# 24 feature weight units split by transfers: the high part cast by one transfer, the low part as minus the high part with the weights added by a second

## The chip, the core and the metric

The kernel runs on one core of a Trainium2 chip. A core has a matrix engine (PE), a vector engine (DVE), a scalar engine (ACT), a general engine (POOL) and an engine that mostly issues transfers (SP). Each of them works through its own list of instructions in order, and waits at an instruction until the semaphores that it names have come. Transfers run beside them on 16 DMA engines, and are issued here from SP's queue and from POOL's.

The metric is the device time of one execution in microseconds (us). Three timed runs of the kernel before took 497.48, 497.65 and 499.13 us; the median is 497.65 us.

## The reference, cut to what matters

Two layers, each a normalisation, one wide projection of 512 tokens, four mixing groups that work on slices of that projection, and one output projection, which is added to the stream. All of it is float32.

```python
def hybrid_layer(x, positions, norm_g, w_in, ...):
    h = rmsnorm(x, norm_g)
    p = h @ w_in
    (cq, ckv, kr, g_a, c_h, c_b, c_c, g_b, sg_u, sg_v, g_c, mq, mk, mv, g_d) = jnp.split(p, offs, axis=-1)
    ...
    o_b = c_b * short_conv(c_c * c_h, conv_w)
    o_c = spatial_gate(sg_u, sg_v, sg_ln_g, sg_ln_b, sg_w, sg_b)
    ...
    y = jnp.concatenate([o_a * jax.nn.silu(g_a), o_b * jax.nn.silu(g_b),
                         o_c * jax.nn.silu(g_c), o_d * jax.nn.silu(g_d)], axis=-1)
    return y @ w_out
```

`w_in` is 1024 x 3488 in each layer. The change concerns the columns of `c_h`, `c_c`, `c_b`, `g_b` and `g_d` (both halves of 128 columns of each) and the second halves of `sg_u` and `g_c`: twelve blocks of 1024 x 128 weights in a layer, 24 in all.

## The kernel before, in words

**Products in two parts.** PE works in a shortened float32 format (fp32r). To keep the precision, each operand is held as a high part (the value rounded to fp32r) and a low part (the value minus its high part), and `mm3` (L254) makes each product of three matrix multiplications: high by high, high by low, low by high.

**Weight units.** The weights come in units (class `Unit`, L271) of up to 128 partitions x 1024 float32, 512 KB. Their order is fixed in `order`: in a layer c0 to c3, uq, ukv, then the list `SEQ` (L338): sq (four units), ga0, ga1, kv (four units), su0, gc0, ch0, cc0, gd0, gd1, cb0, gb0, ch1, cc1, cb1, gb1, su1, gc1; then the units of the output projection (`ZPROD`, L43). A feature unit such as ch0 serves 24 matrix multiplications of 128 x 512, one accumulation over eight slices of 128 rows.

**Loading and splitting.** Two generators go through `order`. `load_units` (L360) takes a raw buffer (there are two, `NRAW`; a few units borrow a buffer of another pool) and issues the load from SP (L265). `split_units` (L378) waits for the load, takes one of six pairs of buffers `whi`, `wlo` (`wS`, L246, `NW`), and for each half of 512 columns makes the high part (a copy on ACT, or on DVE when DVE is well ahead) and the low part (a subtraction on DVE), then gives the raw buffer back. As long as a unit isn't wanted soon (`unit`, L401, marks the next four), a half is only put in where ACT and DVE have nothing planned. A pair of buffers comes free when PE has made its last product with it (`done_unit`, L1338). During the four passes of the kv units (one for each block of 128 tokens) those four units hold four of the six pairs; PE gives them back in the last pass.

**The order of the work.** The program is written by a planner that runs while the kernel is built (class `Order`, L67, class `Chain`, L151). Each piece of work is a generator; the planner keeps a clock of planned time for ACT ("A"), DVE ("V"), POOL ("G") and the DMA engines ("D"), and PE's planned time is `now`. An instruction is put on its engine's list when its inputs are planned to be there (at most 300 ns ahead, `SLACK`), and the planned prices are those in the methods of `Chain`: for instance a transfer issued from SP takes its bytes divided by 360 bytes per ns on the DMA clock, and 2000 ns more until it has landed (L262). At run time the lists are fixed, and an engine whose next instruction isn't ready waits, with all that stands behind it.

**What else stands on the lists near the change.** POOL computes reciprocal roots (`pow_rstd`, L587) and the rotary steps (`rope`, L635) of the token groups, zeroes halves of key tiles (L1204), and issues the transfers of `t_sums` (L318). `t_sums` makes sums of quadrants of the output weights in DRAM in four steps in each layer: a copy issued from SP (L324), then an accumulating transfer issued from POOL (L330). It is spawned at a planned 36 us in the first layer, and after the sq units in the second. The attention heads of the two attention groups (`heads`, L1108) run among the feature units: a product on PE, a maximum on DVE, an exponential on ACT, transposes on PE, a split on ACT and DVE, a product on PE.

Of the kernel before, what the change touches and what calls it, by code (L numbers as in the profile page):

```python
# [11 lines left out]
F32 = mybir.dt.float32  # L12
F32R = mybir.dt.float32r
I32 = mybir.dt.int32
AF = mybir.ActivationFunctionType
ALU = mybir.AluOpType
AX = mybir.AxisListType

P = 128
S = 512  # L20
NT = S // P
D = 1024
# [19 lines left out]
K0, K1, KK = (2, 3, 0, 1), (4, 5, 6, 7), (0, 2, 3, 1)  # L42
ZPROD = ("b11", "t3", "b21", "t4", "t2", "t1", "b22")  # L43
TS0 = 36000.0
TAIL = ((0, 256), (256, 512))

C_CQ, C_KV, C_GA, C_CH, C_CB, C_CC, C_GB = 0, 256, 416, 672, 928, 1184, 1440
# [153 lines left out]
def hybrid_trunk(ctx: ExitStack, tc: tile.TileContext, x, positions, norm_g, w_c, w_f, w_t, w_o, mla_q_norm_g,  # L201
                 mla_w_uq, mla_kv_norm_g, mla_w_ukv, mla_q_g, mla_k_nope_g, mla_k_rope_g, conv_w,
                 sg_ln_g, sg_ln_b, sg_w, sg_b, moba_q_g, moba_k_g, out):
    nc = tc.nc
    V, A, G, PE = nc.vector, nc.scalar, nc.gpsimd, nc.tensor
# [16 lines left out]
    o = Order()  # L222
# [39 lines left out]
    def dma(ch, nbytes, dst, src):  # L262

        o.clk["D"] = max(o.clk["D"], ch.t) + nbytes / 360.0
        nc.sync.dma_start(dst, src)  # L265
        ch.t = o.clk["D"] + 2000.0
# [4 lines left out]
    class Unit:  # L271
        def __init__(self, src, a, b, name):
            self.src, self.a, self.b, self.name = src, a, b, name
            self.loaded, self.ready, self.wanted = Event(), Event(), False
            self.slots = eS if name[:-2] in EARLY else wS

        def view(self):
            n = self.a * self.b
            return (self.hi[:, :n].rearrange("p (a b) -> p a b", a=self.a),
                    self.lo[:, :n].rearrange("p (a b) -> p a b", a=self.a))  # L280
# [15 lines left out]
    def add_unit(*a):  # L296
        u = Unit(*a)
        units[u.name] = u
        u.idx = len(order)
        order.append(u)  # L300
# [8 lines left out]
    tsum_ev = {(l, n, j): Event() for l, n in tsum for j in range(2)}  # L309
# [8 lines left out]
    def t_sums(l):  # L318

        for steps in ((("t1", "b11", "b12"), ("t3", "b12", "b22")), (("t2", "t1", "b22"),), (("t4", "t2", "b21"),)):  # L320
            for n, a, _ in steps:
                for j in range(2):
                    o.clk["D"] = max(o.clk["D"], o.now) + 1500.0
                    nc.sync.dma_start(z_src(l, n, j), z_src(l, a, j))  # L324
                    yield o.now + 4000.0
            yield o.now + 4000.0
            for n, _, b in steps:
                for j in range(2):
                    o.clk["G"] = max(o.clk["G"], o.now) + 1000.0
                    nc.gpsimd.dma_start(z_src(l, n, j), quad(l, b, j), accum_op=ALU.add, max_dma_last_dim=1024)  # L330
                    o.set(tsum_ev[l, n, j], o.now + 10000.0)
                    yield o.now + 4000.0
            yield o.now + 8000.0
# [6 lines left out]
    for l in range(DEPTH):  # L340
# [15 lines left out]
        for half in range(2):  # L356
            for kq in WORDER:
                add_unit(w_o[l, half, kq], 2, 512, f"wo{half}{kq}_{l}")

    def load_units():  # L360
        for u in order:
            ch = Chain(o)
            u.raw_slots = rawS
            if u.name in ("c2_0", "c3_0") or u.name[:-3] in ZPROD and u.name[-3] == "1":
                u.raw_slots = tkS
                u.raw = (yield from tkS.get(ch, f"raw_{u.name}", 96)).rearrange("p a b c -> p (a b c)")
            else:
                u.raw = yield from rawS.get(ch, u.name)
            key = (int(u.name[-1]), u.name[:-3], ord(u.name[-3]) - 48)
            if key in tsum_ev:  # L370
                yield from ch.wait(tsum_ev[key])
            dma(ch, P * u.a * u.b * 4, u.raw[:, :u.a * u.b], u.src)
            o.set(u.loaded, ch.t)
            for e in LOAD_HOOKS.pop(u.name, ()):
                e()
            yield o.now

    def split_units():  # L378
        for u in order:
            ch = Chain(o)  # L380
            yield from ch.wait(u.loaded)
            u.hi, u.lo = yield from u.slots.get(ch, u.name)
            n = u.a * u.b
            for i in range(2):
                while ch.t > o.now + SLACK:
                    yield ch.t - SLACK
                while not u.wanted and max(o.clk["A"], o.clk["V"]) > o.now + WSLACK:
                    yield o.now + 100.0
                sl = slice(i * n // 2, (i + 1) * n // 2)
                c2 = Chain(o, max(o.now, ch.t))  # L390
                hi, lo, raw = u.hi[:, sl], u.lo[:, sl], u.raw[:, sl]
                if o.clk["V"] + 600.0 < o.clk["A"]:
                    yield from c2.dve_fast(V.tensor_copy, hi, raw)
                else:
                    yield from c2.act(A.activation, hi, raw, AF.Copy)
                yield from c2.dve(V.tensor_tensor, lo, raw, hi.bitcast(F32), op=ALU.subtract)
            ch.t = c2.t
            u.raw_slots.put(ch)
            o.set(u.ready, ch.t)
# [890 lines left out]
    def z_out(L, n, i, a, t0, ev, put, c0=0, c1=512):  # L1290

        ch = Chain(o, t0)
        for t, half, op, done in {"t3": ((2 + i, 1, ALU.subtract, False),), "b21": ((i, 0, ALU.add, True),),
                                  "t4": ((2 + i, 0, ALU.add, False),), "t2": ((2 + i, 0, ALU.subtract, True),),
                                  "t1": ((2 + i, 1, ALU.add, True),), "u": ((i, 1, ALU.add, False),),
                                  "b22": ((i, 1, ALU.add, True),)}[n]:
            yield from ch.wait(L.xr[t])
            xx = L.x[t][:, half * 512 + c0:half * 512 + c1]
            k = dict(in0=xx, in1=a[:, c0:c1]) if op == ALU.subtract else dict(in0=a[:, c0:c1], in1=xx)
            yield from ch.dve(V.tensor_tensor, out=xx, op=op, **k)  # L1300
            if done and (c0, c1) != (0, 512):
                nc.sync.dma_start(out[0, t * P:(t + 1) * P, half * 512 + c0:half * 512 + c1], xx)
            elif done:
                if n == "t2":
                    yield from ch.wait(L.s4[i])
                if n in ("t1", "t2") and L.l < DEPTH - 1:
                    junk_ = yield from trS.get(ch, f"jk{t}{half}")
                else:
                    junk_ = a
                yield from row_done(L, t, half, ch.t, junk_)  # L1310
                if n in ("t1", "t2") and L.l < DEPTH - 1:
                    trS.put(ch)
        o.set(ev, ch.t)
        if n == "t4":
            o.set(L.s4[i], ch.t)
        if put:
            put(ch)


    def main():  # L1320
# [21 lines left out]
        def seven(L):  # L1342
# [37 lines left out]
            for n in ZPROD:  # L1380
                for i in range(2):
# [7 lines left out]
                    if (l, n, i) == (DEPTH - 1, "b22", 1):  # L1389
                        ev2 = Event()  # L1390
                        yield from z_out(L, "u", i, a, m.t, ev2, sS.put)
                        for c0, c1 in TAIL:
                            a = yield from accS.get(m, f"ot{c0}_{l}")
# [18 lines left out]
        for L in layers:  # L1412
# [49 lines left out]
            for half in range(0 if L.seven else 2):  # L1462
                us = {}

                def part(t, a, i0, i1, c0=0, c1=512):
                    for i in range(i0, i1):
                        k = YORDER[i]
                        yield from m.wait(L.y[k])
                        if k // 2 not in us:
                            us[k // 2] = yield from unit(m, f"wo{half}{k // 2}_{l}")  # L1470
                        wh, wlo = us[k // 2]
                        yh, yl = y_tiles(L, k)
                        yield from mm3(m, c1 - c0, a[:, c0:c1], yh[:, t * P:(t + 1) * P], yl[:, t * P:(t + 1) * P],
                                       wh[:, k % 2, c0:c1], wlo[:, k % 2, c0:c1], i == 0, i == KT - 1)
                        if t == NT - 1 and c1 == 512 and all(x // 2 != k // 2 for x in YORDER[i + 1:]):
                            done_unit(f"wo{half}{k // 2}_{l}")
                        yield o.now

                acc = {}
                for group, cut in (((0, 1, 2), YCUT), ((3,), 0)) if half == 0 else (((t,), 0) for t in range(NT)):  # L1480
                    for i0, i1 in ((0, cut), (cut, KT)):
                        for t in group:
# [4 lines left out]
                            if (l, half, t) == (DEPTH - 1, 1, NT - 1):  # L1487
                                for c0, c1 in TAIL:
                                    yield from part(t, acc[t], i0, i1, c0, c1)
# [18 lines left out]
    def start():  # L1508
# [27 lines left out]
        LOAD_HOOKS["ukv_0"] = (lambda: load_params(L0),)  # L1536
        L0.par_t = 17500.0
        o.spawn(load_units(), None, 4)
        o.spawn(split_units(), None, 5)
        o.spawn(rope_tables(), ROPET, 6)  # L1540
        o.spawn(main(), None, 10)
# [22 lines left out]
    if 0 in SEVEN:  # L1564
        o.spawn(t_sums(0), TS0, 4)
    o.spawn(start())
# [51 lines left out]
```

## Time and profile before

| what | value |
|---|---|
| timed runs | 497.48, 497.65, 499.13 us, median 497.65 us |
| the profiled execution's own time | 499.12 us |
| its span, from the first to the last instruction | 497.4 us |
| granted clock of PE over it, as a share of the full one | 1.0 |
| hardware queue, issued from SP | 73.10 MB |
| software queue, issued from POOL | 8.39 MB |

The profiled execution's own time is 1.7 us above its span, and 1.5 us above the median of the timed runs.

How to read the lines of the profile that follow. L188 is line 188 of the kernel; since the planner's helpers record nearly all instructions, most of ACT, DVE and POOL stands at L162 and nearly all of PE at L188, and groups are told apart by their tiles ("wlo_cc<-raw_cc,whi_cc" writes a low part from a raw buffer and its high part). Engines: PE (its weight loads are PEld), DVE, ACT, POOL, SP; a "q" behind an engine's name is its queue of issues. Busy PE is the union of modelled matrix multiplications, which overlap, so it can hide short gaps. "Idle before" is the time that the engine stood before instructions of a group, with what ended most of it.

### The profile page before, as it was taken

How to read it: one execution, taken by the hardware profiler on the slowest of the kernel's cores; microseconds unless marked ns; L12 is line 12 of the kernel's file. 1: busy time of each engine (PE TensorE's matmuls, PEld its weight loads, DVE VectorE, ACT ScalarE, POOL GpSimd, SP SyncE). 2: the span in 40 equal slices, each digit the busy share in tenths (PEclk: the TensorE clock that was granted, in tenths of full speed). 3: DMA queues.
4: the chain of work that ended last, by engine and by line, in shares of the span. 5: the costliest groups of instructions: out<-in, count | busy, mean ns of one | idle time of the engine just before them, and what ended most of it. 6: DMA issues, size and time to landing. Idle time of an engine off the chain costs nothing.

```text
span 497.4 us, 7832 instructions
## 1 busy us (share of the span) xinstructions
PE 486.4 (98%) x2448; PEld 412.5 (83%) x2448; DVE 386.0 (78%) x1008; ACT 317.0 (64%) x933; POOL 156.2 (31%) x328
## 2 busy tenths in 40 slices
PE   6899999999999999999999999999999999999997
PEld 4798878788888888888889988888888888888886
DVE  4877884777988788669898698677969788765992
ACT  5688753576777775446657896567758587524640
POOL 6867883656110000000031388463351000000000
PEclk9999999999999999999999999999999999999999
DMA  8545559444575235786474232664548528565642
GB/s 273 150 141 199 196 117 203 171 86 88 192 145 188 71 98 175 210 299 219 157 256 157 86 106 108 211 149 97 118 122 245 142 102 215 174 249 188 227 171 92
DMA packets 35339, 81.98 MB, mean 165 GB/s; under 512 B 7137, under 2 KB 16609, under 8 KB 35042
## 3 DMA queue, kind: packets, MB, share of 16 engines
q1 hardware_dynamic: 26818, 73.10, 42.7%
q0 software_dynamic: 8480, 8.39, 11.5%
q8 instruction: 19, 0.31, 0.3%
q14 instruction: 22, 0.18, 0.1%
HBM read 73.61 MB, written 24.64 MB: 198 GB/s over the span
## 4 chain that ended last, share of the span: by engine, by line
PE 87%; POOL 4%; ACT 3%; DMA 3%; DVE 2%; issue 1%; POOLq 0%; DVEq 0%
PE kv L188 7%; PE cq L188 6%; PE oy L188 6%; PE sq L188 5%; PE cb L188 4%; PE gd L188 4%; PE ch L188 4%; PE cc L188 4%; PE su L188 4%; PE gc L188 4%; PE gb L188 4%; PE ox L188 4%; PE oz L188 4%; PE sa L188 3%; PE ga L188 2%; PE od L188 2%
## 5 line engine op out<-in xcount | busy, mean ns | idle before, releaser
L162 ACT ACTIVATE pd<-pd,mnd 128x256 f32<-128x256 f32 (+3 forms) x50 | 26.9, 547 | 2.8 <-DVE mnd L162 2.3
L330 POOL DMA_DIRECT2D t<-in_w_o_dram x16 | 17.9, 1121 | 33.1 <-DMA t<-t 22.6
L162 ACT ACTIVATE pha<-pTa 128x512 fp32r<-128x512 f32 (+3 forms) x32 | 13.9, 436 | 20.0 <-PE pTa L188 19.8
L188 PE MATMUL kv<-whi_kv,hTh 128*128 128x512 f32 x64 | 26.1, 408 | 0.0
L188 PE MATMUL kv<-whi_kv,hTl 128*128 128x512 f32 x64 | 25.1, 392 | 0.0
L188 PE MATMUL kv<-wlo_kv,hTh 128*128 128x512 f32 x64 | 25.0, 391 | 0.0
L188 PE MATMUL cq<-whi_c,hTh 128*128 128x416 f32 x64 | 24.0, 376 | 0.0
L162 ACT ACTIVATE phd<-pTd 128x512 fp32r<-128x512 f32 (+3 forms) x32 | 13.8, 434 | 14.9 <-PE pTd L188 14.7
L162 ACT ACTIVATE pa<-pa,mna 128x256 f32<-128x256 f32 (+3 forms) x40 | 21.4, 542 | 2.5 <-DVE mna L162 2.4
L188 PE MATMUL cq<-whi_c,hTl 128*128 128x416 f32 x64 | 22.6, 353 | 0.0
L188 PE MATMUL cq<-wlo_c,hTh 128*128 128x416 f32 x64 | 22.5, 351 | 0.0
L162 DVE TENSOR_TENSOR wlo_t<-raw_t,whi_t 128x512 fp32r<-128x512 f32 x32 | 21.1, 691 | 0.0
L162 ACT ACTIVATE whi_t<-raw_t 128x512 fp32r<-128x512 f32 x32 | 18.2, 618 | 4.1 <-DMA raw_t<-t 4.1
L162 POOL TENSOR_SCALAR xss<-xss 128x1 f32<-128x1 f32 x8 | 3.8, 476 | 52.3 <-ACT jk L162 45.1
L162 DVE TENSOR_TENSOR pla<-pTa,pha 128x512 fp32r<-128x512 f32 (+3 forms) x32 | 15.2, 484 | 5.5 <-ACT pha L162 5.5
L188 PE MATMUL sq<-yTh,hTh 128*128 128x512 f32 x48 | 18.9, 393 | 0.0
L188 PE MATMUL sq<-yTh,hTl 128*128 128x512 f32 x48 | 18.7, 390 | 0.0
L162 DVE TENSOR_TENSOR pld<-pTd,phd 128x512 fp32r<-128x512 f32 (+3 forms) x32 | 15.2, 484 | 4.5 <-ACT phd L162 4.4
L188 PE MATMUL sq<-yTl,hTh 128*128 128x512 f32 x48 | 18.7, 390 | 0.0
L162 DVE CUSTOM_DVE_ANT_0 pa<-sa,maskb 128x512 f32<-128x512 f32 (+3 forms) x32 | 14.8, 484 | 5.0 <-PE pTa L188 4.2
L162 DVE TENSOR_TENSOR wlo_b<-raw_b,whi_b 128x512 fp32r<-128x512 f32 x24 | 16.0, 688 | 0.7 <-ACT whi_b L162 0.7
L162 DVE CUSTOM_DVE_ANT_0 pd<-sd,maskb 128x256 f32<-128x256 f32 (+3 forms) x32 | 15.0, 483 | 2.0 <-PE pTd L188 1.9
(377 smaller groups left out, 1853.0 us busy)
## 6 DMA issues: line engine op xcount, KB each, us to landing
t<-in_w_o_dram POOLq DMA_DIRECT2D x16, 512.0 KB, 6.2
raw_t<-t SPq DMA_DIRECT2D x16, 512.0 KB, 4.0
raw_b<-in_w_o_dram SPq DMA_DIRECT2D x12, 512.0 KB, 4.2
raw_sq<-in_w_t_dram SPq DMA_DIRECT2D x8, 512.0 KB, 3.5
t<-in_w_o_dram SPq DMA_DIRECT2D x8, 512.0 KB, 4.4
raw_kv<-in_w_t_dram SPq DMA_DIRECT2D x8, 512.0 KB, 3.6
t<-t SPq DMA_DIRECT2D x8, 512.0 KB, 4.8
ys<-ysc SPq DMA_DIRECT2D x14, 256.0 KB, 5.2
```

Of the source, the lines that this page charges most:

```text
L162: f(*a, **k)
L188: f(*a, **k)
L330: nc.gpsimd.dma_start(z_src(l, n, j), quad(l, b, j), accum_op=ALU.add, max_dma_last_dim=1024)
```

## The change

Units whose name is in a new list `BY_DMA` (twelve names, so 24 units in the two layers) are no longer loaded into a raw buffer from SP, and no longer split by copies and subtractions. `load_units` skips them. `split_units` takes the pair of buffers for such a unit in its turn, as before, and starts a generator `unit_by_dma` for it. That issues, from POOL, a transfer of the weights from DRAM straight into `hi`, casting float32 to fp32r on the way; when it is planned to have landed, one ACT instruction writes minus `hi` into `lo` (128 x 1024, where before there were halves); then POOL issues a second transfer of the same weights, which is added onto `lo`. The planner's prices for these are in `pool_dma`: 1000 ns on POOL's clock for an issue, the bytes divided by 360 bytes per ns on the DMA clock (twice the bytes for the accumulating one), and 2500 ns until it has landed. The wait for `t_sums` in `load_units` moves to a helper, `sum_done`, unchanged in what it does; the units in `BY_DMA` never have such a wait.

```diff
+BY_DMA = ("ch0", "cc0", "gd0", "gd1", "cb0", "gb0", "ch1", "cc1", "cb1", "gb1", "su1", "gc1")
...
             self.slots = eS if name[:-2] in EARLY else wS
+            self.by_dma = name[:-2] in BY_DMA
...
+    def sum_done(ch, u):
+        key = (int(u.name[-1]), u.name[:-3], ord(u.name[-3]) - 48)
+        if key in tsum_ev:
+            yield from ch.wait(tsum_ev[key])
+
+    def pool_dma(ch, nbytes, *a, **k):
+
+        yield from ch._emit("G", 1000.0, nc.gpsimd.dma_start, a, k)
+        o.clk["D"] = max(o.clk["D"], ch.t) + nbytes / 360.0
+        ch.t = o.clk["D"] + 2500.0
+
+    def unit_by_dma(u, ch):
+
+        n = u.a * u.b
+        hi, lo = u.hi[:, :n], u.lo[:, :n]
+        yield from sum_done(ch, u)
+        yield from pool_dma(ch, P * n * 4, hi, u.src)
+        yield from ch.act(A.activation, lo, hi.bitcast(F32), AF.Copy, scale=-1.0)
+        yield from pool_dma(ch, 2 * P * n * 4, lo, u.src, accum_op=ALU.add, max_dma_last_dim=4096)
+        o.set(u.ready, ch.t)
+
     def load_units():
         for u in order:
+            if u.by_dma:
+                continue
             ch = Chain(o)
...
-            key = (int(u.name[-1]), u.name[:-3], ord(u.name[-3]) - 48)
-            if key in tsum_ev:
-                yield from ch.wait(tsum_ev[key])
+            yield from sum_done(ch, u)
             dma(ch, P * u.a * u.b * 4, u.raw[:, :u.a * u.b], u.src)
...
     def split_units():
         for u in order:
             ch = Chain(o)
+            if u.by_dma:
+                u.hi, u.lo = yield from u.slots.get(ch, u.name)
+                o.spawn(unit_by_dma(u, ch), None, 4)
+                continue
             yield from ch.wait(u.loaded)
```

## The prediction

> **What bounds the kernel now.** I read the page first, for its busy shares and its chain of waits.
>
> ```profile
> span 497.4 us, 7832 instructions
> ...
> PE 486.4 (98%) x2448; PEld 412.5 (83%) x2448; DVE 386.0 (78%) x1008; ACT 317.0 (64%) x933; POOL 156.2 (31%) x328
> ...
> q1 hardware_dynamic: 26818, 73.10, 42.7%
> q0 software_dynamic: 8480, 8.39, 11.5%
> ...
> PE 87%; POOL 4%; ACT 3%; DMA 3%; DVE 2%; issue 1%; POOLq 0%; DVEq 0%
> ```
>
> PE is busy for 98% of the span, and the chain that ends last lies on PE for 87%. The second view is the list of PE's waits; it is short enough to show whole.
>
> ```profile
> PE hT L188 <- DVE h L162: 3.9, 3, 2.2
> PE warm L1516 <- DVE ones L162: 1.3, 1, 1.3
> PE t0a L188 <- DVE Q L162: 1.1, 1, 1.1
> PE cT L188 <- DVE ct L162: 0.6, 1, 0.6
> PE mp L188 <- ACT vnh L162: 0.3, 1, 0.3
> PE ng L188 <- DMA gz<-in_norm_g_dram: 0.2, 1, 0.2
> ```
>
> That is 7.4 us in all (the first number of each row), and no row names a feature weight unit. The third view is the busy time by stage. I cut the span where the changed units live: the end of the kv units with the first feature units (98 to 126 us), the rest of the first layer's features, the same two stages in the second layer, and the end. Columns are PE, PEld, DVE, ACT and POOL, then granted clock, DMA share and GB/s.
>
> ```profile
> 98.00:126.00 28.00, 28.00 (x161) 24.28 (x160) 22.01 (x73) 19.11 (x62) 14.74 (x44) 1.00 0.42 92
> 126.00:204.00 78.00, 78.00 (x413) 65.97 (x412) 65.16 (x166) 53.80 (x127) 4.83 (x7) 1.00 0.48 141
> 354.00:374.00 20.00, 20.00 (x114) 17.10 (x113) 14.38 (x43) 12.57 (x37) 7.78 (x18) 1.00 0.56 134
> 374.00:444.00 70.00, 70.00 (x352) 58.68 (x351) 57.20 (x139) 45.34 (x103) 4.08 (x5) 1.00 0.63 192
> ```
>
> In all four, PE is busy the whole time. So whatever the change takes from DVE and ACT is work beside a busy PE. A busy PE can hide short gaps, because its products overlap in this view; the groups by shape bound those.
>
> ```profile
> L188 PE MATMUL gd<-hTh,whi_gd 128*128 128x512 f32 x32 | 13.5, 422 | 0.0
> L188 PE MATMUL ch<-hTh,whi_ch 128*128 128x512 f32 x32 | 13.4, 418 | 0.0
> ...
> L188 PE MATMUL gd<-hTh,wlo_gd 128*128 128x512 f32 x32 | 12.6, 393 | 0.0
> L188 PE MATMUL ch<-hTh,wlo_ch 128*128 128x512 f32 x32 | 12.6, 393 | 0.0
> ```
>
> The first product of each three is 25 to 29 ns longer than the one with the low part. These are the two largest such excesses among the changed names; (25 + 29) / 2 x 32 = 0.9 us for four units, so at most 5.2 us for 24 units could be hidden stalls. That bounds any gain in these stages.
>
> **The change part by part. Removed:** two copies and two subtractions for each unit.
>
> ```profile
> L162 ACT ACTIVATE whi_kv<-raw_kv 128x512 fp32r<-128x512 f32 x16 | 9.7, 623 | 0.0
> ...
> L162 ACT ACTIVATE whi_cc<-raw_cc 128x512 fp32r<-128x512 f32 x8 | 5.0, 627 | 0.0
> ...
> L162 ACT ACTIVATE whi_ukv<-raw_ukv 128x256 fp32r<-128x256 f32 x4 | 1.7, 414 | 0.0
> ```
> ```profile
> L162 DVE TENSOR_TENSOR wlo_cc<-raw_cc,whi_cc 128x512 fp32r<-128x512 f32 x8 | 5.5, 685 | 0.0
> ```
>
> For 24 units that is 48 x 0.627 = 30 us of copies (a few of them on DVE) and 48 x 0.685 = 33 us of DVE. All of it lies beside the busy PE shown above, so I take 0 for it; the bounds are 0 and the 5.2 us of hidden gaps. The 24 loads that leave SP's list take nothing off the path either: SP computes nothing, and what moves up behind them is the t_sums copies, which are early enough already.
>
> **Added on ACT:** 24 times minus the high part, 128 x 1024. From 256 columns (414 ns) to 512 (623 ns) a column costs 0.82 ns, so 1024 columns are estimated at 1.04 us, 25 us in all, against 30 us of copies. Taken alone this is 0. What is new is a wait: before, a unit was loaded well ahead of its copies (no "idle before" in the cc row); now ACT's instruction is put in 0.3 us ahead of the planned landing of the first transfer. If that lands late, ACT stands, and behind it exponentials and splits of the attention heads.
>
> **Added on POOL:** 48 issues. The nearest are the accumulating transfers of t_sums, the same bytes:
>
> ```profile
> L330 POOL DMA_DIRECT2D t<-in_w_o_dram x16: 1006/1093/1624, 66.9 to 415.6; - x16
> ...
> DMA to landing us min/median/max: 5.5/6.2/11.4
> ```
>
> At a median of 1.09 us, 48 issues are 52 us of POOL. From 126 us and from 374 us on POOL is nearly idle (4.83 of 78 and 4.08 of 70 us), so there they cost nothing by themselves. They collide at 98 to 126 and 354 to 374 us, where the four kv units give back their buffers and four changed units start at once: 8 issues, 8.7 us, in front of or among the last rotary steps of the MoBA keys. The slack there is read from the end of those steps to the first MoBA score product on the chain:
>
> ```profile
> 120.03 0.47 POOL L162 TENSOR_TENSOR mk<-mk,rbmk 128x32 f32<-128x32 f32 x2
> ```
> ```profile
> 367.00 0.46 POOL L162 TENSOR_TENSOR mk<-mk,rbmk 128x32 f32<-128x32 f32 x2
> ```
> ```profile
> 143.60 1.04 PE sd L188 x6
> ...
> 380.07 1.04 PE sd L188 x6
> ```
>
> 23 us in the first layer, 12.6 us in the second; less 8.7 us, some 14 and 4 us remain, part of which the key transposes and splits use. So I take 0, with up to 3 us in the second layer as its upper bound.
>
> **The first transfer against its planned landing.** The planner gives it 1.0 + 0.13 + 524288/360 ns + 2.5 = 5.1 us from the issue. No row shows a cast into SBUF. Below it is bounded by the plain load from SP (raw_gd: 3.5 us for the same bytes, plus POOL's issue of 1.1 instead of 0.3, so 4.3 us), above by the accumulating one (6.2, worst 11.4).
>
> ```profile
> raw_gd<-in_w_f_dram SPq DMA_DIRECT2D x4, 512.0 KB, 3.5
> ```
>
> It reads and writes what raw_gd does, so alone I take 4.3 us, which is in time: 0 for the 16 units that start one by one.
>
> The Trainium skill ("DMA: Bandwidth & Descriptors", "Anatomy of one DMA — SWDGE (gpsimd) path") gives such transfers 2.0 us plus their bytes over 436 GB/s, so 3.2 us here; by that estimate even the bursts would be in time and the sum would be nothing. The rows above with 5.5 us at the least for transfers of that path disagree with it, though they accumulate in DRAM.
>
> **The bursts.** Four units start within the last kv pass. The planner books 4 x (1.46 + 2.91) = 17.5 us on the DMA clock. The queues' shares give what transfers really occupy: 42.7% x 497.4 us for 73.10 MB is 1.52 us for 512 KB on the hardware queue; 11.5% x 497.4 us over the 16 large transfers is 3.6 us each on the software queue. With 3.6 us for each accumulation and 1.52 to 3.6 us for each cast a burst needs 20.5 to 28.8 us, 3 to 11 us more than planned, and ACT is made to wait for that, in parts. What such a wait costs PE has happened once in this trace, when the load of su0 came late:
>
> ```profile
> 84.92 1.16 ACT L162 ACTIVATE whi_su<-raw_su 128x512 fp32r<-128x512 f32 x2 [6.05 <-DMA raw_su<-in_w_f_dram]
> ```
> ```profile
> 93.97 0.32 PE L188 MATMUL t0a<-ident,Q 128*96 128x128 f32 x1 [1.13 <-DVE Q L162]
> ```
>
> The chain of waits joins the two: the load, then rotary steps on POOL, then DVE's Q, then PE. 6.05 us on ACT became 1.13 us on PE, 0.19 for one. I take one such loss for each burst (6 us lies inside 3 to 11), 2.3 us; bounds 0, and 22 us if all 11 us reach PE twice.
>
> **Sum:** 499.12 (the profiled execution's own time) + 0 + 0 + 2.3 = 501.4 us. That execution lies 1.5 us above the median of the runs, so against the median the forecast is 499.9 us.
>
> **The rivals.** No measurable change, 497.7 us: the casts land as the planner has it, or ACT's idle time takes the waits (78 - 53.8 = 24 us of idleness from 126 to 204 us, spread over the heads). For it: PE waits for nothing in these stages. Against: this slack is shared with the heads' own chains, and the bursts fall together with other traffic.
>
> Late everywhere: the cast is as slow as the accumulating transfer, and 24 units come 6.2 - 5.1 = 1.1 us late, 26 us of ACT waits. At 0.19 that is 5 us, at one for one 26 us; at the middle, 0.45, some 12 us: 509.5 us. It begins to decide once casts land later than 5.1 us when alone. For it: the 11.4 us worst case. Against: a median late by only 1.1 us.
>
> Faster: DVE is busy 65.16 of 78 us among the first layer's heads; with 33 us less, maxima and splits come sooner and the hidden gaps shrink. Half of the 5.2 us would give 495.0 us. It decides if the 25 ns excess is waiting for DVE rather than PE's own change of operands. Against: the waits of PE show no row for it.
>
> POOL as a blocked queue: in the second layer it stood 15 us before a t_sums transfer, and now the issues of later units would stand behind that.
>
> ```profile
> 407.62 1.01 POOL L330 DMA_DIRECT2D t<-in_w_o_dram  x1 [15.34 <-DMA t<-t]
> ```
> ```profile
> 402.36 0.33 SPq L265 DMA_DIRECT2D raw_cb<-in_w_f_dram  x1
> 402.78 0.48 SPq L324 DMA_DIRECT2D t<-t  x1
> ```
> ```profile
> 438.92 5.44 PE gb L188 x24
> ```
>
> Its copy was issued directly behind a raw load of cb1, which the change removes, so this wait shrinks; and a unit's buffers come five units ahead, at least 5 x 5.44 = 27 us, more than the 15 us. It would cost PE only beyond that; I count it with the late case. That the cast might not round, so that the low part is nothing, would change precision and not the time.
>
> **How the numbers follow.** 0.3% (1.5 us) is about what a measurement of this kernel can tell from no change: 496.2 to 499.1 us. Chances: bursts 0.38 (499.9 us, own range 499.1 to 503), no change 0.35, late everywhere 0.14, faster 0.13. So slower 0.38 + 0.14 = 0.52. The range, 496.5 to 508 us, takes in no change, the bursts with the 3 us of POOL, and part of the late case; some 0.1 is left out on each side.
>
> **What would show it.** Right: waits of ACT at the new minus-high instructions of ch0, cc0, gd0 and gd1 and their second-layer twins, some us each, a wait of PE of about 1 us behind each burst, and none at the other 16. Casts that land 4 to 5 us after their issue when alone speak for my price, 6 us and more for the late case. If ACT shows no such wait, or PE's list stays at 7.4 us, the forecast falls to no change; if the first products fall to some 393 ns, the faster case was right. A new order of PE's list that makes or removes a wait like that at t0a, far from the changed units, would also prove the forecast wrong.

## The result, and the profile after

The changed kernel takes 501.94 us (median of four runs, 500.95 to 502.41), the kernel before 497.56 us (four runs, 497.47 to 499.13) on the same chip. The ratio is 1.0077, 95% interval 1.0062 to 1.0091: slower by 4.4 us. The forecast was 499.9 us.

First the page of the changed kernel, the lines that answer to those of before; its profiled execution took 502.41 us by its own time:

```profile
span 500.7 us, 7810 instructions
...
PE 489.2 (98%) x2448; PEld 414.4 (83%) x2448; DVE 362.1 (72%) x969; ACT 313.3 (63%) x906; POOL 187.8 (38%) x370
...
q1 hardware_dynamic: 23362, 60.51, 35.3%
q0 software_dynamic: 15392, 33.56, 32.8%
```

The work moved as the diff says. DVE lost 24 us of busy time, ACT 4, POOL gained 32, and 12.6 MB left SP's queue (73.10 to 60.51) while 25.2 MB came to POOL's (8.39 to 33.56). None of that explains a longer span by itself. PE's list of waits, 7.9 us in all against 7.4 before, says where to look:

```profile
PE hT L189 <- DVE h L163: 3.0, 2, 2.5
PE mixT L189 <- DVE pla L163: 2.8, 1, 2.8
PE warm L1543 <- DVE ones L163: 1.3, 1, 1.3
PE cT L189 <- DVE ct L163: 0.5, 1, 0.5
PE mp L189 <- ACT vnh L163: 0.3, 1, 0.3
```

One row is new, 2.8 us before the transposes "mixT"; the 1.1 us at t0a has gone, and the row of hT is 0.9 us shorter. The busy time by stage, in the same cuts as before, says where the new row lies:

```profile
98.00:126.00 28.00, 28.00 (x156) 23.85 (x155) 18.55 (x70) 19.05 (x57) 19.39 (x47) 1.00 0.97 213
...
354.00:374.00 20.00, 17.17 (x86) 14.11 (x86) 10.03 (x35) 11.35 (x32) 7.46 (x19) 0.91 0.93 292
```

The end of the kv units in the first layer, where the first four changed units start together, has PE busy throughout. Its twin in the second layer has not: 2.83 of 20 us are missing, and the granted clock over these 20 us is 0.91. The DMA share rose in both, from 0.42 to 0.97 and from 0.56 to 0.93.

What PE waited for is followed back in the timelines of PE, DVE and SP (start, duration, and in brackets the idle time with what ended it), with the landing time of the store from its own view:

```profile
368.69 0.66 PE L189 MATMUL mixT<-ident,mix 128*128 128x128 f32 x4 [2.83 <-DVE pla L163]
...
352.44 0.42 DVE L163 TENSOR_TENSOR yaa<-yaa 128x256 f32<-128x256 f32 x1
367.36 0.68 DVE L163 TENSOR_TENSOR yaa<-oa,oba 64x512 f32<-64x512 f32 x1 [6.12 <-DMA ysc<-yaa]
...
358.79 0.33 SPq L266 DMA_DIRECT2D raw_t<-t  x1
359.17 0.48 SPq L885 DMA_DIRECT2D ysc<-yaa  x1
...
DMA to landing us min/median/max: 8.1/8.1/8.1
```

"yaa" is the y tile of the first pair of attention heads. The second pair writes into the same buffer, so DVE may not start on it before the store of the first pair's tile to DRAM ("ysc<-yaa", L885) has landed. The tile was finished at 352.9 us; its store was issued at 359.17, directly behind a load of a t_sums block ("raw_t<-t"), and landed 8.1 us later. DVE stood 6.12 us, the split "pla" behind it was late, and PE stood. The same three steps in the kernel before:

```profile
356.04 0.42 DVE L162 TENSOR_TENSOR yaa<-yaa 128x256 f32<-128x256 f32 x1
...
356.49 0.33 SPq L858 DMA_DIRECT2D ysc<-yaa  x1
...
DMA to landing us min/median/max: 2.6/2.6/2.6
```

There the store went out as soon as the tile was done and landed after 2.6 us; DVE's next write into the tile, at 364.62 us, came 5.6 us after that. The changed kernel finishes the tile 3.6 us earlier and has it in DRAM 8 us later. Two delays make that up: 6.3 us in front of SP's issue, and 5.5 us more of landing.

The first delay has its row in SP's list of waits (us in total, times, longest), and the groups of SP's issues say why it is new (min/median/max duration, first and last start); before first, then after, which has two rows:

```profile
L265 SPq DMA_DIRECT2D raw_t<-t x16: 319/323/384, 194.8 to 470.5; - x16
```
```profile
L266 SPq DMA_DIRECT2D raw_t<-t x16: 319/326/697, 127.0 to 474.9; - x16
...
SPq L266 <- DMA t<-in_w_o_dram: 8.6, 1, 8.6
```

SP stood 8.6 us at that load, for the accumulating transfer of t_sums that makes what it reads. Before, these loads began at 194.8 us in the first layer, and the first of the second layer was issued at 435.8 us; now they begin at 127.0 and 349.4. With the 24 loads gone, SP fills its two raw buffers 68 and 86 us earlier with units of the output projection, meets blocks that aren't summed yet, and stands, with the store of y behind it.

The second delay is traffic. Windows around the store, one of before, in which the store was in flight, and four of after (the last three columns are granted clock, DMA share and GB/s):

```profile
354.00:361.00 7.00, 7.00 (x40) 6.05 (x39) 5.86 (x18) 4.94 (x19) 1.41 (x3) 1.00 0.55 150
```
```profile
354.00:361.00 7.00, 7.00 (x40) 6.03 (x40) 5.96 (x25) 5.88 (x22) 2.96 (x7) 1.00 1.16 317
361.00:365.00 4.00, 4.00 (x22) 3.30 (x21) 0.23 (x1) 2.28 (x6) 2.25 (x5) 1.00 1.06 283
365.00:369.00 4.00, 1.17 (x7) 0.68 (x6) 1.64 (x4) 0.00 (x0) 0.00 (x0) 1.00 1.03 419
369.00:374.00 5.00, 5.00 (x22) 4.10 (x21) 2.20 (x7) 3.18 (x5) 2.25 (x7) 0.66 0.43 163
```

From the store's issue to its landing the DMA engines are full (1.03 to 1.16); before they were busy for 0.55 of the window of its store, and for 0.20 of the next four microseconds. The last row has a second loss: behind the gap PE is "busy", but at a clock of 0.66, so 0.34 x 5.00 = 1.7 us are lost there. Together, 2.8 + 1.7 and less the 1.1 us at t0a, that is 3.4 us; the spans differ by 500.7 - 497.4 = 3.3 us, so in this execution little else is missing. The 0.9 us at hT don't count: in this execution the granted clock is also down to 0.50 at 12 to 14 us, and what PE no longer waits there it spends in slower products (its third group of hT products starts at 14.83 us, before at 14.94).

### The profile page after: what moved, and what is told of

Its sections match the earlier page's. It is cut to its first block, busy times and chain, and to the rows that moved or that the text cites. A ratio compares the mean times of both kernels' runs of the same rounds, so it can differ in the third digit from the quotient of the medians.

```text
span 500.7 us, 7810 instructions
## 1 busy us (share of the span) xinstructions
PE 489.2 (98%) x2448; PEld 414.4 (83%) x2448; DVE 362.1 (72%) x969; ACT 313.3 (63%) x906; POOL 187.8 (38%) x370
## 3 DMA queue, kind: packets, MB, share of 16 engines
q1 hardware_dynamic: 23362, 60.51, 35.3%
q0 software_dynamic: 15392, 33.56, 32.8%
## 4 chain that ended last, share of the span: by engine, by line
PE 88%; POOL 4%; DMA 3%; ACT 3%; DVE 2%; issue 1%; POOLq 0%; DVEq 0%
PE kv L189 10%; PE oy L189 6%; PE cq L189 6%; PE sq L189 5%; PE gd L189 4%; PE cc L189 4%; PE cb L189 4%; PE ch L189 4%; PE gb L189 4%; PE ox L189 4%; PE oz L189 4%; PE gc L189 4%; PE su L189 3%; PE ga L189 3%; PE sa L189 3%; PE sd L189 2%
## 5 line engine op out<-in xcount | busy, mean ns | idle before, releaser
L163 ACT ACTIVATE pd<-pd,mnd 128x256 f32<-128x256 f32 (+3 forms) x43 | 22.7, 540 | 2.0 <-DVE mnd L163 1.9
```

The costliest lines, as they stand in the source:

```text
L163: f(*a, **k)
```

## Experiments

Each kernel was timed in five rounds beside the kernel before on the same chip; ratios are to that.

**Is the store's wait the loss?** The second pair's y tile gets a buffer of another pool, so that nothing waits for the store. The order on every engine is unchanged. The kernel before got the same edit as a control.

```diff
+    ytS = Slots(o, 1, lambda name: None)
...
-            H.ya_box[0] = yield from yaS.get(ch, f"ya{H.name}")
+            yield from ytS.get(ch, "")
+            H.ya_box[0] = (wk.tile([P, S], F32, tag="ya", name=f"ya{H.name}") if h == 0 else
+                           (yield from hS.get(ch, f"ya{H.name}"))[:, 0:S])
```

> The changed kernel with the same order of instructions on every engine; only the y tile of the second pair of heads lies in another buffer, so that DVE need not wait until the first pair's y tile has been stored to DRAM. Theory (late store): the change loses its time where DVE waits 6.1 us for that store in the second layer and PE 2.8 us behind it, and in the cut of PE's clock after it. Then the wait of PE before the mixT transposes goes, the granted clock stays at 1.0 there, and the time is 497.3 to 498.3 us, a ratio to before of 1.000 +- 0.002. Rival (the forecast's): ACT stands at the new minus-high instructions; then the buffer changes nothing, 501.5 to 502.5 us, 1.008. Rival (traffic everywhere): each of many late landings costs a little; then at most 1 us comes back, 501 us.

> The kernel before with the same second buffer and the same order: the control. In its profile no instruction waits for that store, so every theory expects the time of before, a ratio of 1.000 +- 0.002.

Measured: 499.27 us, ratio 1.0023 (1.0005 to 1.0041), against 1.0008 (0.9994 to 1.0022) for the control. The wait at mixT is gone, with the traffic as it was (DMA share 1.02 to 1.15 from 354 to 369 us). The changed kernel itself wasn't run beside these two; its ratio was 1.0077 above and is 1.0100 below. So the wait for the store, with what follows from it, is most of the loss. What is left shows as one new row in PE's list, at 373.9 us:

```profile
PE tmkd L189 <- POOL mk L163: 0.9, 1, 0.9
```

**Which of the two delays?** Three kernels, each with one part taken away. In the first each accumulating transfer of a unit moves 64 of its 1024 columns; in the second the t_sums additions of the second layer do; in the third the stores of y in the second layer are issued from ACT's queue.

```diff
-        yield from pool_dma(ch, 2 * P * n * 4, lo, u.src, accum_op=ALU.add, max_dma_last_dim=4096)
+        yield from pool_dma(ch, 2 * P * n * 4, lo[:, 0:64], u.src[:, 0:64], accum_op=ALU.add, max_dma_last_dim=4096)
```

> The changed kernel with the same order of instructions on every engine, but each accumulating transfer moves only 64 of its 1024 columns (left out: the weights that are added to the other columns of the low parts, which stay minus the high part). Theory 'traffic' (the loss is the store of the first y tile of the second layer, late because all transfers together are more than the DMA engines carry at 350 to 370 us): the store lands 3 to 5 us after its issue instead of 8.1, DVE's wait of 6.1 us for it falls to under 2.5, PE's wait of 2.8 us at mixT is gone, the ratio to the kernel before is 0.999 to 1.002. Rival 'queue' (the store is late because a raw load of 512 KB stands directly ahead of it on SP's own queue, whatever the other queues carry): the store still lands after 7 to 8 us and the ratio stays at 1.006 to 1.008.

```diff
-                    nc.gpsimd.dma_start(z_src(l, n, j), quad(l, b, j), accum_op=ALU.add, max_dma_last_dim=1024)
+                    c = slice(0, 64 if l else 1024)
+                    nc.gpsimd.dma_start(z_src(l, n, j)[:, c], quad(l, b, j)[:, c], accum_op=ALU.add, max_dma_last_dim=1024)
```

> The changed kernel, but in the second layer the transfers that accumulate the t_sums in DRAM move only 64 of their 1024 columns (left out: those sums in the other columns). One such transfer is in flight from 349.7 to 358.7 us in the changed kernel, directly ahead of the burst. Theory 'traffic': it takes some 3.6 us of the DMA engines off a stretch that is full from 354 to 369 us, so the store lands 2 to 4 us earlier, DVE's wait falls from 6.1 to 2 to 4 us, PE's wait of 2.8 us at mixT to 0 to 1, ratio 1.000 to 1.004. Rival 'queue': the store lands after 7 to 8 us as before, ratio 1.006 to 1.008. If it is the casts and additions alone that fill the engines, also 1.006 to 1.008, but with the raw load ahead of the store landing earlier.

```diff
-                nc.sync.dma_start(ysc[L.l][kt], yv)
+                (nc.scalar if L.l else nc.sync).dma_start(ysc[L.l][kt], yv)
```

> The changed kernel with the same order of work on PE, DVE and POOL; in the second layer the stores of the y tiles are issued by ACT, on its own queue, instead of by SP. Theory 'traffic': the first store of the second layer still lands 6 to 8 us after its issue, because all queues share the DMA engines; DVE waits 4 to 6 us for it, PE 1 to 3 us at mixT, ratio 1.005 to 1.008. Rival 'queue': the store no longer stands behind the raw load on SP's queue and lands after 2.5 to 3.5 us as in the kernel before; the wait at mixT is gone, ratio 0.999 to 1.003.

Measured, with the store's row in each, in this order (duration of the issue, its start, then issue to landing, and who waited):

```profile
L885 SPq DMA_DIRECT2D ysc<-yaa x1: 424/424/424, 359.1 to 359.1; - x1
...
  DVE yaa L163: 2.7, 1
...
DMA to landing us min/median/max: 6.1/6.1/6.1
```
```profile
L886 SPq DMA_DIRECT2D ysc<-yaa x1: 424/424/424, 356.1 to 356.1; - x1
...
DMA to landing us min/median/max: 5.7/5.7/5.7
```
```profile
L885 ACTq DMA_DIRECT2D ysc<-yaa x1: 347/347/347, 357.5 to 357.5; - x1
...
  DVE yaa L163: 3.0, 1
...
DMA to landing us min/median/max: 7.6/7.6/7.6
```

- Small additions: 1.0022 (1.0013 to 1.0032). SP is blocked as long as before (359.1), the landing takes 2 us less. That was a little less than expected (6.1 us, not 3 to 5), and enough: no wait at mixT.
- Small t_sums: in the profiled execution SP is released 3.1 us earlier, because the addition that it stands at is done earlier; the store lands at 361.8 and nobody waits. The ratio of all runs, 1.0059 (1.0039 to 1.0080), is above what was expected of traffic (up to 1.004) and above what that profile shows; its six runs go from 499.66, which is the profiled one, to 503.32 us. This run shows the block on SP, and doesn't price it.
- Store from ACT: 1.0020 (1.0012 to 1.0029). On a queue of its own the store still takes 7.6 us, so its slowness is traffic, not its place behind a 512 KB load; but it is issued 1.7 us earlier, and that also is enough.

Neither theory was right alone. The store has two delays of about 6 us each, the block in front of SP and the slow landing, and in the first and third run some 2 us off either of them were enough to free PE.

**What is left over, 1.0 us at tmkd?** In the run with the store on ACT, POOL's timeline has the six rotary instructions of the last MoBA key tile with four issues between them (the row of PE last):

```profile
368.54 0.46 POOL L163 TENSOR_TENSOR rbmk<-mk,sinT 128x32 f32<-128x32 f32 x2 [3.39 <-DVE mk L163]
...
369.97 0.90 POOL L163 DMA_DIRECT2D wlo_cc<-in_w_f_dram  x1 [0.65 <-ACT wlo_cc L163]
...
370.91 1.09 POOL L163 DMA_DIRECT2D wlo_gd<-in_w_f_dram  x1
...
372.02 1.11 POOL L163 DMA_DIRECT2D wlo_gd<-in_w_f_dram  x1
372.60 1.10 POOL L163 DMA_DIRECT2D whi_gb<-in_w_f_dram  x1
373.17 0.81 POOL L163 TENSOR_TENSOR mk<-mk,rbmk 128x32 f32<-128x32 f32 x1
...
374.03 0.33 PE L189 MATMUL tmkd<-ident,mk 128*128 128x128 f32 x1 [0.97 <-POOL mk L163]
```

In the kernel before the six follow each other without a gap, from 366.03 to 367.46 us:

```profile
366.03 0.47 POOL L162 TENSOR_TENSOR rbmk<-mk,sinT 128x32 f32<-128x32 f32 x2 [1.94 <-DVE mk L162]
```

Six instructions that took 1.43 us take 5.4 us, and they begin 2.5 us later, behind DVE. The next kernels run these six on DVE, with the planner's times unchanged: with the stores on ACT, in the changed kernel alone, and with the buffer of the first experiment. The changed kernel ran once more beside them.

```diff
-                yield from ch.pool(G.tensor_tensor, out_, in0, in1, op=op)
+                yield from ch.pool((V if name == "mk31" else G).tensor_tensor, out_, in0, in1, op=op)
```

> The changed kernel as it is, once more, so that the two runs beside it have it on the same chip. Both theories: DVE waits 5 to 7 us for the store of the first y tile of the second layer, PE 2.5 to 3.2 us at mixT, ratio to the kernel before 1.006 to 1.009; no row of ACT waiting for a cast in the second layer over 1 us.

> As the run with the stores issued by ACT, and in addition the six rotary instructions of the last MoBA key tile of the second layer run on DVE instead of POOL (the order on PE, ACT and SP is the same, DVE has six short instructions more). Theory 'issues' (what is left, ratio 1.002, is PE's wait of 1.0 us at tmkd, because POOL issues four transfers among these six instructions): the wait at tmkd is gone, PE's list of waits has no row that the kernel before hasn't, ratio 0.999 to 1.001. Rival 'spread' (what is left lies in small waits elsewhere, or in more traffic everywhere): the wait at tmkd is gone, yet the ratio stays at 1.0015 to 1.003.

> The changed kernel with the rotary instructions of that key tile on DVE, the stores left with SP. Theory 'the two losses lie one behind the other and the longer covers the shorter': DVE still waits about 6 us for the store and PE about 2.8 us at mixT, the ratio stays within 0.001 of that of the changed kernel on the same chip (1.006 to 1.009). Rival 'the losses add up': 0.002 less, 1.004 to 1.006.

> Both cures at once in the changed kernel, the stores left with SP: the second pair's y tile in a buffer of its own, so that DVE needn't wait for the store, and the rotary instructions of the last MoBA key tile of the second layer on DVE. Theory 'these two waits are the whole loss': no wait of PE at mixT or tmkd, ratio 0.999 to 1.001. Rival 'something is left that no wait of these two shows': both waits gone, ratio 1.0015 to 1.003, as in the run with the stores on ACT and the rotary steps on DVE.

Measured:

| kernel | median us | ratio, interval | PE at mixT / tmkd in the profiled execution, us |
|---|---|---|---|
| changed kernel again | 503.08 | 1.0100 (1.0081 to 1.0119) | 1.9 / 0.9 |
| rotary steps on DVE | 502.38 | 1.0080 (1.0067 to 1.0093) | 3.1 / none |
| rotary steps on DVE, stores on ACT | 499.14 | 1.0018 (1.0007 to 1.0030) | none / none |
| rotary steps on DVE, own buffer | 498.72 | 1.0006 (0.9996 to 1.0016) | none / none |

The last row closes the account. Its list of PE's waits, whole, and its store:

```profile
PE hT L189 <- DVE h L163: 2.8, 2, 2.2
PE warm L1548 <- DVE ones L163: 1.3, 1, 1.3
PE cT L189 <- DVE ct L163: 0.6, 1, 0.6
PE mp L189 <- ACT vnh L163: 0.3, 1, 0.3
```
```profile
L886 SPq DMA_DIRECT2D ysc<-yaa x1: 493/493/493, 359.4 to 359.4; - x1
...
DMA to landing us min/median/max: 8.1/8.1/8.1
```

The store is as late as in the changed kernel, the DMA engines as full, POOL issues as much; with nobody waiting for either, the time can't be told from that of the kernel before. So by this route the two waits are the whole of the loss that can be measured. Three things stay open. What the second wait costs by itself: taking it away changed 1.0023 to 1.0006 with the buffer, 1.0020 to 1.0018 with the stores on ACT and 1.0100 to 1.0080 with neither, and in each pair the intervals overlap; nor was the kernel before run with the rotary steps on DVE, though its list has no wait at tmkd that they could take away. Whether the two waits add up or the longer covers the shorter: the rerun has 1.9 + 0.9 us, in its fastest execution, and the run without the second 3.1 us in one piece. And why the run with the stores on ACT stays at 1.0018: its profiled execution was its slowest, with 2.4 us of waiting for a load in the first microseconds, and doesn't show the cause.

**Does the forecast's own mechanism exist?** Two kernels with another order: one leaves the four units of the burst to SP, ACT and DVE; one keeps all 24 by transfers, but holds SP's loads of later units back until the changed units ahead of them have their buffers, so that SP can't run ahead.

```diff
-BY_DMA = ("ch0", "cc0", "gd0", "gd1", "cb0", "gb0", "ch1", "cc1", "cb1", "gb1", "su1", "gc1")
+BY_DMA = ("cb0", "gb0", "ch1", "cc1", "cb1", "gb1", "su1", "gc1")
```

> The change for 16 units only: ch0, cc0, gd0 and gd1, which start together at the end of the kv units, are loaded and split as before. Theory (the burst makes the store late): no burst, the store lands in 3 to 5 us, PE's wait in the second layer goes; 497.3 to 498.5 us, ratio 1.000 to 1.002. Rival (traffic everywhere): two thirds of the loss stay, 500.5 us, 1.005. Rival (SP's list runs ahead): SP still skips 16 loads, but the ones before cb0 hold it back until later; about the same as the theory, told apart by the next run.

```diff
             if u.by_dma:
+                yield from Chain(o).wait(u.taken)
                 continue
...
                 u.hi, u.lo = yield from u.slots.get(ch, u.name)
+                o.set(u.taken, o.now)
```

> The change for all 24 units, but the loads that stand behind them on SP's list are held back until the changed unit before them has its buffers, so that SP does not run ahead with loads of the output weights. Theory A (the burst of casts and accumulations alone fills the DMA engines): the store still takes 6 to 8 us, the time stays at 500.5 to 502 us. Theory B (the output weights' load directly ahead of the store in SP's queue makes it late): the store takes 3 to 5 us, the wait goes, 497.3 to 498.5 us.

Measured: 1.0135 (1.0113 to 1.0156) and 1.0138 (1.0107 to 1.0169), both slower than the change itself. ACT, DVE and PE of the first:

```profile
164.34 1.06 ACT L163 ACTIVATE wlo_cb<-whi_cb 128x1024 fp32r<-128x1024 f32 x1 [5.19 <-DMA whi_cb<-in_w_f_dram]
...
165.91 0.69 DVE L163 SCALAR_TENSOR_TENSOR th_gd<-th_gd,gd 128x512 f32<-128x512 f32 x1 [5.38 <-ACT th_gd L163]
...
167.20 0.76 PE L189 MATMUL tmkd<-ident,mk 128*128 128x128 f32 x4 [4.09 <-DVE pld L163]
```

That is the forecast's chain link by link, in the first layer, at cb1, one of the 16 units that I had priced at nothing: its cast was issued at 148.86 and landed at 164.32 us, beside two t_sums additions that took 10.8 and 16.9 us. The held kernel has the same wait (4.4 us on ACT, 3.6 on PE). In the changed kernel this cast took 12.2 us and landed at 162.01 us, but ACT came to it only at 162.32 us and didn't wait. In the second layer of the held kernel the t_sums loads are issued at 419 us instead of 349, the store goes out at 357.16, and there is no wait at mixT, though it still lands after 7.7 us. In that layer of the kernel without the burst the store lands after 2.2 us, and there is no wait at mixT either. So both orders cure the one place, and another opens.

**Is it ACT's early place?** The run without the burst again, with 9.0 us instead of 2.5 booked behind a transfer's bytes:

```diff
-        ch.t = o.clk["D"] + 2500.0
+        ch.t = o.clk["D"] + 9000.0
```

> Sixteen units by transfers (without ch0, cc0, gd0, gd1), as in the run without bursts, but the planner books 9.0 us instead of 2.5 us of landing time behind the bytes, so ACT's minus-high instructions are put in 6.5 us later among ACT's work. Theory 'place' (the loss of that run, ratio 1.0135, is ACT's 5.2 us wait at the minus-high of cb in the first layer, which came from a planned time too early): ACT's waits for casts sum to under 1 us, PE's wait of 4.1 us behind it is gone, ratio 1.000 to 1.003. Rival 'work' (16 units by transfers cost time by themselves, wherever ACT takes them up): the ratio stays above 1.008, with the wait at another place.

Measured: 501.00 us, 1.0055 (1.0043 to 1.0067). ACT waits for no cast any more and the 4.1 us of PE are gone, as "place" has it; yet the ratio is above its 1.003, with 1.6 us of small waits of PE at 400 to 409 us that weren't there. Their cause was not followed up. Nor does this kernel still compute the layers' output, for a reason that was not found, so it shows neither theory, and nothing below rests on it.

## Why the prediction was right, and where it was not

**Direction, bound and range: right, the number in part by luck.** Slower was forecast at 0.52; 501.94 us lies in the range. PE was the bound and stayed it. But the waits that the 2.3 us were made of didn't come: by the prediction's own signs its mechanism was wrong, since ACT has no wait for the casts of ch0, cc0, gd0 and gd1 in either layer, and the wait at t0a went. A wait that the sum doesn't have took their place.

**The removed work at 0: right.** DVE is busy 24 us less (the estimate was 33; the 48 subtractions are gone, and the planner gave DVE other work, for instance 7 of the 50 rescalings of pd that ACT had), and the time of the last kernel in the table equals that of the kernel before. The copies and subtractions were hidden. The first products did get shorter in the changed kernel (gd 422 to 414 ns, ch 418 to 407), which gave nothing that can be measured.

**"What moves up behind them is the t_sums copies, which are early enough already": this step failed.** I looked at what leaves SP's list and asked only whether the rest is early enough. What moved up is the loads of t_sums blocks, by 68 and 86 us, and these wait for an addition; behind them, in the same list, stands a store that has a deadline. It took SP out for 8.6 us.

**The price of a cast alone, 4.3 us: right.** The two casts of su1, which run nearly alone, and the two pairs of gd in the first and the second burst, from issue to landing:

```profile
DMA to landing us min/median/max: 4.1/4.2/4.3
```
```profile
DMA to landing us min/median/max: 5.0/5.1/5.2
```
```profile
DMA to landing us min/median/max: 6.9/7.9/8.9
```

The estimate by the rate of the Trainium skill ("DMA: Bandwidth & Descriptors", "Anatomy of one DMA — SWDGE (gpsimd) path") was 3.2 us; the first row disagrees by 1 us, the others by more.

**"0 for the 16 units that start one by one": the value right for this kernel, the reason wrong.** The price alone isn't what most casts paid. 15 of the 24 landed more than 6 us after their issue (6.3 to 12.2), and 11 of these are among the 16 outside the bursts; the planner has 5.1. Yet ACT waited for only one; to the others it came after they had landed. That lateness is what the case "late everywhere" spoke of; it cost next to nothing on ACT, and it was the store that the full DMA engines made late.

**The bursts: half right.** There are two, and the first layer's casts land after 4.0 to 5.2 us, about the 5.1 planned, so it costs nothing. My 20.5 to 28.8 us of DMA time for one was too much: if the additions of t_sums occupy the engines as before, the software queue's share gives an estimate of (32.8% x 500.7 - 11.5% x 497.4) / 24 = 4.5 us for one unit, 17.8 us for four, nearly the planner's 17.5. The burst of the second layer, whose casts land after 6.5 to 9.3 us, is the place of the loss; a t_sums addition and loads of the output weights fall together with it there.

**Who waits: wrong for this kernel.** Waits of ACT at the new minus-high instructions were to be seen at eight units; ACT waited for one cast, 2.7 us at a unit outside the bursts, without cost. The waiter was DVE, for a store that the change doesn't touch. The forecast's chain exists, as two other orders showed; which of the late transfers hurts depends on what the planned order puts behind it.

**The size: 4.4 us instead of 2.3.** Not 1.13 us twice but 2.8 us once (6.12 us on DVE became 2.83 us on PE, 0.46 for one, where I had taken 0.19 from ACT), 1.7 us from the lower clock behind it in the profiled execution, and in other executions POOL's wait below. The 1.1 us at t0a, from which I took the price, was absent from the profiled execution after.

**POOL's issues in the second layer, "0, with up to 3 us": the place right, the value not settled.** There is a wait at tmkd, of 0.9 to 1.3 us in five of the profiled executions, though not in the first one of the changed kernel; what it adds to the time lies within the intervals. I had set 8 issues against a slack of 4 us; four issues stood between the last rotary steps themselves. The 48 issues took 38 us in all, not 52: 0.5 to 0.9 us for a cast, 0.8 to 1.6 for an accumulation. The block of 15 us at t_sums shrank to nothing, as argued. The minus-high instruction took 1.05 us for an estimated 1.04.

## What to carry to other kernels

When transfers are taken out of an in-order queue, list what moves up: a load that now comes long before its data exists stops the queue, and the stores and loads behind it are late. When work goes from compute engines to transfers, look for the waits that a full DMA stage lengthens, above all for stores that must land before their buffer is used again; a second buffer for one tile undid most of this loss. The relief of engines that a busy PE already hid was worth nothing here, so the change could only lose by its side effects.

## What the runs showed of the hardware that was not expected

**The clock behind a gap of PE.** The row of 369 to 374 us above has 0.66 behind a gap of 2.83 us. Gaps of other runs, with the window behind each: the rotary steps on DVE (3.05 us), the run without the burst (4.09).

```profile
369.90 0.66 PE L189 MATMUL mixT<-ident,mix 128*128 128x128 f32 x4 [3.05 <-DVE pla L163]
...
369.00:374.00 5.00, 4.10 (x23) 3.53 (x24) 3.70 (x13) 2.37 (x5) 0.73 (x1) 1.00 0.65 220
```
```profile
169.00:174.00 5.00, 5.00 (x21) 4.13 (x20) 3.98 (x7) 4.11 (x7) 1.42 (x2) 0.80 0.37 68
```

2.83 us was punished and 3.05 us was not; nor was the held kernel's 3.57, nor the rerun's 1.87. At the start of the program it happens behind shorter ones: in six of the fourteen profiled executions, the changed kernel's among them, the clock falls to 0.50 for some microseconds at 11 to 15 us, behind gaps of 1.3 to 2.5 us; the kernel before has one of 2.2 us there and keeps 1.00. In these runs the length alone doesn't decide. The Trainium skill ("TensorE: Matmul & The Clock Gate", "Part 1: The HAM clock gate") has a free-running window of 3.4 us, after an idle one of which the clock falls to half. By these figures one window at half the clock costs an estimated 1.7 us, which agrees with the 1.7 us lost in the first row; that the place of the gap in the windows matters would fit the gaps that went unpunished; that a gap of 2.83 us, shorter than a window, is enough does not.

**Casts and accumulating transfers in company.** The t_sums additions of 512 KB land after a median of 8.6 us in the changed kernel against 6.2 before, and took up to 16.9 us in the run without the burst. A cast of 512 KB took 3.7 to 4.3 us at best and up to 12.2 us in the changed kernel, 15.5 us in the run without the burst. The store of the first y tile of the second layer (256 KB) landed after 2.2 to 2.6 us in the four profiled executions that have no burst of casts there, and after 5.7 to 8.5 us in the ten that have one, from SP's queue and from ACT's alike.
